# One table load for both blocks' norms, and Newton steps one slot later, in a decoder block on one NeuronCore

## The chip, the cores and the metric

The kernel runs on one core of one Trainium2 chip. The metric is the device time of one execution in microseconds, the lower the better. TensorE multiplies, ScalarE applies activation functions (each function needs its table in the engine, and a table is brought in by an ACT_TABLE_LOAD in ScalarE's own queue), VectorE and GpSimd do elementwise work, and SyncE issues every DMA of this kernel.

## The reference, cut to what matters

One layer over 2048 positions of 1024 features: a norm and an input projection into two token mixers (gated linear attention and a short convolution), an output projection with residual, and then the part that this change touches:

```
def rmsnorm(x, g):
    y = xf * lax.rsqrt(jnp.mean(xf * xf, axis=-1, keepdims=True) + NORM_EPS)
    return (y * g).astype(x.dtype)
...
        x = x + mixed
        h2 = rmsnorm(x, norm2_g[l])
        ffn = (jax.nn.silu(h2 @ w_ffn_gate[l]) * (h2 @ w_ffn_up[l])) @ w_ffn_down[l]
        x = x + ffn
    return rmsnorm(x, norm_f_g)
```

All of it is float32; D_FF is 2816.

## The kernel before, in words

**Tiling.** Features lie on partitions (128 of them, 8 tiles), positions on the free axis in four blocks of 512. The FFN goes over two halves of two blocks each: `ffn_up(0)`, `ffn_down(0)`, `ffn_up(1)`, `ffn_down(1)`. In `ffn_up` a step m (11 of them) makes two units, one for the gate weights and one for the up weights.

**A unit** (L370) multiplies a 2 by 2 matrix of weight tiles with a 2 by 2 matrix of operand tiles with seven products instead of eight (Strassen and Winograd). Every float32 value is split into a high and a low part (`split`, L152: ScalarE copies the high part, L153, VectorE subtracts to get the low one, L154), and each product takes 12 matmuls in `ffn_up`: four feature tiles times high·high, high·low and low·high (L366 to L368). The third matmul of a product is the first that needs the low half of its weights. The seven weight combinations are named A11, S1, S2, A12, S3, S4 and A22, in the order in which their splits are written (L343); GpSimd makes the sums (L349 to L356). Results stay in PSUM and ScalarE (L386) and VectorE (L390) take them out. The last product, with A22, adds onto the bank of the product with S3, so that it can start only when VectorE has read that bank into the tile called c22. Four buffers hold split weights, eight PSUM banks are shared by everything.

**Order of the work.** Each engine runs its queue strictly in the order in which the program's scheduler put it. `tick` (L201) is called after every product: every second tick gives one step to the background list (in `ffn_up` the splits and stores of the activations, `split_later`), and of the ticks between, every second one gives a step to the list `ahead`. One such step is called a slot here; it comes every four products.

**The norms made beside the projections** are steps of `ahead`:

- `h2_ahead` (L864), beside `ffn_up(0)`: the second norm of the two blocks of half 1. For block j after two slots each, `psum_rstd` (L175) multiplies the squares' sums with a matrix of ones on TensorE (`tot`), and `finish_rstd` (L182) takes Ln (L184) and Exp (L185) on ScalarE for a first guess y0 of the inverse root, scales `tot` on VectorE (L186), and improves the guess with a Newton step, three VectorE instructions (`newton`, L162: L163 to L165). The result lies in PSUM as `rb_ps`. Then `combine` makes the operands of half 1.
- `finish_later` (L976), beside `ffn_up(1)`: the final norm of the two blocks of half 0. For each block: eight slots that load a tile and add its square (`sum_squares`, L770), one `psum_rstd`, eight slots that load, scale (L992) and store a tile.

The Silu of the gate units (`silu`, L420, instruction L422) needs another table than Ln and Exp.

Of the kernel before, what the change touches and what calls it, by code (L numbers as in the profile page):

```python
# [10 lines left out]
F32 = mybir.dt.float32  # L11
F32R = mybir.dt.float32r
U32 = mybir.dt.uint32
AF = mybir.ActivationFunctionType
ALU = mybir.AluOpType
# [3 lines left out]
P = 128  # L19
D = 1024  # L20
SEQ = 2048
PB = 512
# [9 lines left out]
EPS = 1e-6  # L32
# [14 lines left out]
C_G1, C_G2, C_GF, C_BG, C_GN, C_CW = 0, 8, 16, 24, 26, 27  # L47
# [4 lines left out]
def tile_hymba_block(ctx, tc, x, xt, win, wa, wgu, wout, wffn, wdown, wdown_first, small, out):  # L52
    nc = tc.nc
    act, dve, pool, pe = nc.scalar, nc.vector, nc.gpsimd, nc.tensor

    def pool_of(name, bufs, **kw):
        return ctx.enter_context(tc.tile_pool(name=name, bufs=bufs, **kw))
# [6 lines left out]
    tiny = pool_of("tiny", 2)  # L64
# [11 lines left out]
    ones = const.tile([P, P], F32, name="ones")  # L76
# [8 lines left out]
    eps = const.tile([P, 1], F32, name="eps")  # L85
# [46 lines left out]
    def col(c):  # L132
        return sml[:, c : c + 1]

    def bank(name="mm"):
        return ps.tile([P, PB], F32, name=name, tag="mm")

    def tt(name):
        return tp.tile([P, PB], F32, name=name, tag="t")

    def bt(name, shape=(P, PB)):
        return bx[0].tile(list(shape), F32, name=name, tag="b")

    def load(dst, src):
        return nc.sync.dma_start(dst, src)

    def store(dst, src):
        return nc.sync.dma_start(dst, src)
# [13 lines left out]
    def newton(y, v, l, y0):  # L162
        dve.tensor_tensor(l, y0, y0, ALU.mult)  # L163
        dve.scalar_tensor_tensor(l, l, -0.5, v, ALU.mult, ALU.mult)
        dve.scalar_tensor_tensor(y, l, 1.5, y0, ALU.add, ALU.mult)  # L165
# [6 lines left out]
        finish_rstd(rb, tot, n)  # L172
        return rb

    def psum_rstd(ssq, n):  # L175

        tot, rb = bank("tot"), bank("rb_ps")
        pe.matmul(tot[:], ones[:], ssq[:], start=True, stop=True)
        finish_rstd(ssq, tot, n, rb)
        return rb  # L180

    def finish_rstd(v, tot, n, rb=None):  # L182
        l, y0 = bt("l"), bt("y0")
        act.activation(l[:], tot[:], AF.Ln, bias=eps[:], scale=1.0 / n)  # L184
        act.activation(y0[:], l[:], AF.Exp, scale=-0.5)  # L185
        dve.tensor_scalar(v[:], tot[:], 1.0 / n, EPS, ALU.mult, ALU.add)  # L186
        newton((v if rb is None else rb)[:], v[:], l[:], y0[:])
# [227 lines left out]
        act.activation(s[:], c[:], AF.Copy)  # L415
        return s

    last_silu = []

    def silu(c, in_psum):  # L420
        s = tt("sg") if in_psum else c
        last_silu[:] = [act.activation(s[:], c[:], AF.Silu)]  # L422
        return s


# [170 lines left out]
    def in_proj(half, ops, first=None, differences=None):  # L596
# [20 lines left out]
        for i0 in (0, 2):  # L617
            for r, j, c, p in next(units):
                store(s_g[2 * half + j][i0 + r][:], silu(c, p)[:])
# [150 lines left out]
    def sum_squares(ssq, y, first):  # L770
        if first:
            act.activation(ssq[:], y, AF.Square)
        else:
            q = tt("q")
            act.activation(q[:], y, AF.Square)  # L775
            pool.tensor_tensor(ssq[:], ssq[:], q[:], ALU.add)  # L776

    def build_mix(half):
        def pair(b, k):
            return load_pair(s_gla[b][:, k] if k < HEADS else s_mix[b][k - HEADS])  # L780

        return [[pair(2 * half + j, k) for j in range(2)] for k in range(KD)]
# [81 lines left out]
    def h2_ahead(ssq):  # L864


        rb = []
        for j in range(2):
            for _ in range(2):
                yield  # L870
            rb.append(psum_rstd(ssq[j], D))

        def put(n, k, h):
            store_split(s_h2p[n][k], h)

        yield from combine(lambda k, j: s_x1[2 + j][k][:], C_G2, rb, put)
# [34 lines left out]
    def store_split(dst, y):  # L911
        o = bx[1].tile([P, 2, PB], F32R, name="so", tag="so")
        split(y[:], o[:, 0, :], o[:, 1, :])
        store(dst[:], o[:].bitcast(F32))
# [6 lines left out]
    def ffn_down(half):  # L921
# [51 lines left out]
        if half == 0:  # L973
            ahead[:] = [finish_later(half)]

    def finish_later(half):  # L976

        for j in range(2):
            ssq = tiny.tile([P, PB], F32, name="ssx0", tag="ssx0", bufs=1)
            for d in range(KD):  # L980
                y = bt("y")
                load(y[:], s_x1[2 * half + j][d][:])
                yield
                sum_squares(ssq, y[:], d == 0)
            yield
            act.preload_act_table_set("natural_log_exp_and_others")
            rb = psum_rstd(ssq, D)
            for d in range(KD):
                y = bt("y")
                load(y[:], s_x1[2 * half + j][d][:])  # L990
                yield
                dve.scalar_tensor_tensor(y[:], y[:], col(C_GF + d), rb[:], ALU.mult, ALU.mult)  # L992
                store(out[2 * half + j, :, d, :], y[:])

    def last_unit(src, ops, b12, y, ssq):
# [71 lines left out]
    ssq = out_proj(0, build_mix(0))  # L1067
    drain_background(lambda: (3, PT - 1) in done)
    h2 = no_operands()
    ssq = out_proj(1, build_mix(1), h2_first(ssq, h2), h2_rest(h2))  # L1070
    ahead.append(h2_ahead(ssq))
    mixing.close()
    bx[:] = [
# [112 lines left out]
```

## Time and profile before

| | |
|---|---|
| runs of the kernel | 2110.91 us median of 3 (2108.93 to 2113.38) |
| profiled execution | span 2109.1 us from its first to its last instruction; no other time is recorded of it |
| TensorE busy | 2033.1 us, 96% |
| VectorE busy | 1418.4 us, 67% |
| ScalarE busy | 1014.1 us, 48% |
| GpSimd busy | 972.4 us, 46% |
| mean granted TensorE clock | 0.992 of full |

A row of the waits names the engine and line that stood still, the engine and line that ended it, and then the total in us, the number of times and the longest one. A row of the timeline gives start, duration, engine, line, operation and tiles, and in brackets the idle time before it and who ended it. A row of the windows gives, after the stretch, the busy us of TensorE, of its weight loads, of VectorE, ScalarE and GpSimd, each with the number of instructions, then the granted clock, the DMA share and GB/s. In the profile TensorE is PE, VectorE DVE, ScalarE ACT, GpSimd POOL.

### The profile page before, as it was taken

To read this page: it belongs to the slowest core of one execution; us is meant where nothing else is said; L and a number is where in the kernel's file an instruction comes from. 1 tells how busy PE (TensorE), PEld (TensorE's weight loads), DVE (VectorE), ACT (ScalarE), POOL (GpSimd) and SP (SyncE) were. 2 spreads that over 40 slices of the span, in tenths; PEclk is the share of its full clock that TensorE was granted. 3 is DMA by queue.
4 is the path that set the end of the run, shared out by engine and by line. 5 is a ranking of instruction groups with operands and counts; after the bars stand their busy time and mean duration, and the time that the engine had idled before them with its cause. 6 is when DMAs were issued, how large, how long until landed. Compare 5 with 4: busy or idle time off the path is not lost.

```text
span 2109.1 us, 26874 instructions
## 1 busy us (share of the span) xinstructions
PE 2033.1 (96%) x9133; PEld 1648.9 (78%) x9133; DVE 1418.4 (67%) x1983; ACT 1014.1 (48%) x1997; POOL 972.4 (46%) x703
## 2 busy tenths in 40 slices
PE   5999999999999999999999999999999989999996
PEld 4778888877888878788888878787888868877775
DVE  7669786549753786788786665554766666665564
ACT  5555455656542356445545443333554554543344
POOL 3436322222102464564464348764645544436774
PEclk9999999999999999999999999999999999999998
DMA  7349485425586872656545687697454535587763
GB/s 277 126 158 318 139 329 164 148 83 164 201 284 235 325 249 100 241 198 221 217 172 220 243 327 272 235 338 296 158 207 179 206 134 190 183 344 281 269 269 110
DMA packets 189241, 464.43 MB, mean 220 GB/s; under 512 B 19824, under 2 KB 65072, under 8 KB 179504
## 3 DMA queue, kind: packets, MB, share of 16 engines
q1 hardware_dynamic: 189104, 462.72, 60.4%
q8 instruction: 72, 1.18, 0.2%
q14 instruction: 65, 0.53, 0.1%
HBM read 297.49 MB, written 165.15 MB: 219 GB/s over the span
## 4 chain that ended last, share of the span: by engine, by line
PE 70%; DVE 8%; DMA 7%; ACT 3%; issue 3%; POOL 2%; SPq 0%; DVEq 0%; ACTq 0%; POOLq 0%
PE mm L366 21%; PE mm L368 21%; PE mm L367 21%; DVE wq L154 2%; DMA op<-shT 1%; DVE so L154 1%; PE mm L794 1%; DVE h L490 1%; PE mm L795 1%; PE mm L797 1%; DVE op L154 1%; DMA sx<-y 1%; ACT wq L153 1%; PE o_ps L718 1%; DMA shT<-so 1%
## 5 line engine op out<-in xcount | busy, mean ns | idle before, releaser
L366 PE MATMUL mm<-op,wq 128*128 128x512 f32 x2499 | 981.3, 395 | 23.8 <-DVE c L390 7.8
L368 PE MATMUL mm<-op,wq 128*128 128x512 f32 x2499 | 966.1, 392 | 12.6 <-DVE wq L154 11.9
L367 PE MATMUL mm<-op,wq 128*128 128x512 f32 x2499 | 976.0, 391 | 0.0
L154 DVE TENSOR_TENSOR wq<-raw,wq 128x512 fp32r<-128x512 f32 (+2 forms) x626 | 527.3, 849 | 329.9 <-ACT wq L153 324.3
L153 ACT ACTIVATE wq<-raw 128x512 fp32r<-128x512 f32 (+2 forms) x626 | 363.6, 587 | 555.8 <-PE mm L368 402.4
L366 PEld LDWEIGHTS mm<-op,wq 128*128 128x128 f32 x2499 | 470.8, 188 | 137.6 <-ACT wq L153 12.3
L368 PEld LDWEIGHTS mm<-op,wq 128*128 128x128 f32 x2499 | 470.5, 188 | 123.5 <-DVE wq L154 24.8
L367 PEld LDWEIGHTS mm<-op,wq 128*128 128x128 f32 x2499 | 471.2, 189 | 96.7 <-issue 1.0
L351 POOL TENSOR_TENSOR raw<-s,raw 128x512 f32<-128x512 f32 (+2 forms) x97 | 127.5, 1314 | 422.2 <-DVE wq L154 402.0
L390 DVE TENSOR_TENSOR c<-mm,c 128x512 f32<-128x512 f32 x267 | 183.0, 686 | 95.7 <-PE mm L368 93.0
L349 POOL TENSOR_TENSOR s<-raw 128x512 f32<-128x512 f32 (+2 forms) x97 | 130.2, 1343 | 216.2 <-DMA raw<-in_wffn_dram 88.8
L356 POOL TENSOR_TENSOR raw<-raw 128x512 f32<-128x512 f32 (+2 forms) x97 | 126.7, 1306 | 135.3 <-DVE wq L154 128.1
L386 ACT ACTIVATE c<-mm 128x512 f32<-128x512 f32 x267 | 154.7, 585 | 38.0 <-PE mm L368 36.8
L776 POOL TENSOR_TENSOR ssx<-ssx,q 128x512 f32<-128x512 f32 x52 | 76.5, 1483 | 156.0 <-ACT q L775 155.8
L350 POOL TENSOR_TENSOR raw<-raw 128x512 f32<-128x512 f32 (+2 forms) x97 | 135.1, 1393 | 4.1
L965 POOL TENSOR_TENSOR y<-c,y 128x512 f32<-128x512 f32 x66 | 98.7, 1499 | 49.0 <-DVE c L390 46.6
L154 DVE TENSOR_TENSOR so<-t,so 128x512 fp32r<-128x512 f32 x100 | 91.2, 918 | 25.9 <-ACT so L153 25.4
L153 ACT ACTIVATE wq<-s 128x512 fp32r<-128x512 f32 (+2 forms) x97 | 56.9, 586 | 93.5 <-PE mm L368 83.3
L794 PE MATMUL mm<-op,wq 128*128 128x512 f32 x256 | 100.9, 395 | 0.0
L795 PE MATMUL mm<-op,wq 128*128 128x512 f32 x256 | 99.8, 390 | 0.0
L154 DVE TENSOR_TENSOR wq<-s,wq 128x512 fp32r<-128x512 f32 (+2 forms) x97 | 84.1, 867 | 15.6 <-ACT wq L153 15.0
L153 ACT ACTIVATE so<-t 128x512 fp32r<-128x512 f32 x100 | 62.5, 627 | 41.8 <-DMA sa_T<-so 16.1
(177 smaller groups left out, 1885.0 us busy)
## 6 DMA issues: line engine op xcount, KB each, us to landing
raw<-in_wffn_dram SPq DMA_DIRECT2D x44, 1024.0 KB, 5.7
sa_T<-so SPq DMA_DIRECT2D x88, 512.0 KB, 5.3
op<-sa_T SPq DMA_DIRECT2D x88, 512.0 KB, 9.2
sa_B<-so SPq DMA_DIRECT2D x69, 512.0 KB, 3.4
op<-sa_B SPq DMA_DIRECT2D x69, 512.0 KB, 9.0
raw<-in_win_dram SPq DMA_DIRECT2D x23, 1024.0 KB, 5.5
raw<-in_wdown_dram SPq DMA_DIRECT2D x24, 768.0 KB, 6.2
sx<-y SPq DMA_DIRECT2D x48, 256.0 KB, 3.2
```

Of the source, the lines that this page charges most:

```text
L153: last_hi[:] = [act.activation(hi, src, AF.Copy)]
L154: return dve.tensor_tensor(lo, src, hi.bitcast(F32), ALU.subtract)
L349: pool.tensor_tensor(s1, a21, a22, ALU.add)
L350: pool.tensor_tensor(a21, a11, a21, ALU.subtract)
L351: pool.tensor_tensor(a11, s1, a11, ALU.subtract)
L356: pool.tensor_tensor(a12, a12, a11, ALU.subtract)
L366: pe.matmul(o[:], wh, xh, start=first and k == 0, stop=False, skip_group_check=True)
L367: pe.matmul(o[:], wh, xl, start=False, stop=False, skip_group_check=True)
L368: return pe.matmul(o[:], wl, xh, start=False, stop=k == n - 1, skip_group_check=True)
L386: act.activation(t[:], o[:], AF.Copy)
L390: dve.tensor_tensor(t[:], o[:], t[:], ALU.add)
L794: pe.matmul(o[e, j][:], wh, m[:, 0, :], start=k == 0, stop=False)
```

## The change

`psum_rstd` goes, and `both_rstd` treats the two blocks together: two `tot` products, one load of the table that holds Ln and Exp (asked for behind the last Silu issued), two Ln, two Exp and two scalings; then one slot of `ahead` passes, and then come both Newton steps. Every Ln, Exp and later Silu is tied behind the one before it, so that the scheduler can't mix them. `h2_ahead` waits three slots and does both blocks in the fourth and fifth, where the old one did them in the third and fifth. `finish_later` sums the squares of both blocks first (16 slots), makes both norms, and then scales both blocks; the second block's factor waits in SBUF and is copied by ScalarE into a PSUM bank when its turn comes.

```
-    def psum_rstd(ssq, n):
-        tot, rb = bank("tot"), bank("rb_ps")
-        pe.matmul(tot[:], ones[:], ssq[:], start=True, stop=True)
-        finish_rstd(ssq, tot, n, rb)
-        return rb
+    def both_rstd(ssq, rb):
+        tot = [bank("tot") for _ in range(2)]
+        for j in range(2):
+            pe.matmul(tot[j][:], ones[:], ssq[j][:], start=True, stop=True)
+        l, y0 = [[bt(n) for _ in range(2)] for n in ("l", "y0")]
+        with tc.issue_after(last_silu[0].ins):
+            last_exp[:] = [act.preload_act_table_set("natural_log_exp_and_others")]
+        for j in range(2):
+            with tc.issue_after(last_exp[0].ins):
+                last_exp[:] = [
+                    act.activation(l[j][:], tot[j][:], AF.Ln, bias=eps[:], scale=1.0 / D)
+                ]
+        for j in range(2):
+            with tc.issue_after(last_exp[0].ins):
+                last_exp[:] = [act.activation(y0[j][:], l[j][:], AF.Exp, scale=-0.5)]
+        for j in range(2):
+            dve.tensor_scalar(ssq[j][:], tot[j][:], 1.0 / D, EPS, ALU.mult, ALU.add)
+        yield
+        for j in range(2):
+            newton((rb[j] or ssq[j])[:], ssq[j][:], l[j][:], y0[j][:])
...
     def silu(c, in_psum):
         s = tt("sg") if in_psum else c
-        last_silu[:] = [act.activation(s[:], c[:], AF.Silu)]
+        with ExitStack() as stack:
+            if last_exp:
+                stack.enter_context(tc.issue_after(last_exp[0].ins))
+            last_silu[:] = [act.activation(s[:], c[:], AF.Silu)]
...
     def h2_ahead(ssq):
-        rb = []
-        for j in range(2):
-            for _ in range(2):
-                yield
-            rb.append(psum_rstd(ssq[j], D))
+        for _ in range(3):
+            yield
+        rb = [bank("rb_ps") for _ in range(2)]
+        yield from both_rstd(ssq, rb)
...
     def finish_later(half):
+        ssq = [
+            tiny.tile([P, PB], F32, name=f"ssx{j}", tag=f"ssx{j}", bufs=1) for j in range(2)
+        ]
         for j in range(2):
-            ssq = tiny.tile([P, PB], F32, name="ssx0", tag="ssx0", bufs=1)
             for d in range(KD):
                 y = bt("y")
                 load(y[:], s_x1[2 * half + j][d][:])
                 yield
-                sum_squares(ssq, y[:], d == 0)
-            yield
-            act.preload_act_table_set("natural_log_exp_and_others")
-            rb = psum_rstd(ssq, D)
+                sum_squares(ssq[j], y[:], d == 0)
+        yield
+        rb = [bank("rb_ps"), None]
+        yield from both_rstd(ssq, rb)
+        for j in range(2):
+            if j:
+                rb[1] = bank("rb_ps")
+                act.activation(rb[1][:], ssq[1][:], AF.Copy)
             for d in range(KD):
                 y = bt("y")
                 load(y[:], s_x1[2 * half + j][d][:])
                 yield
-                dve.scalar_tensor_tensor(y[:], y[:], col(C_GF + d), rb[:], ALU.mult, ALU.mult)
+                dve.scalar_tensor_tensor(y[:], y[:], col(C_GF + d), rb[j][:], ALU.mult, ALU.mult)
                 store(out[2 * half + j, :, d, :], y[:])
```

In the built programs TensorE has 8869 matmuls and transposes and SyncE 1233 DMAs, before and after; ScalarE has 1911 instructions before and 1904 after: eight table loads fewer and one copy more. The order moves at three places.

**First place, ScalarE beside `ffn_up(0)`,** where the second of the two h2 norms was. In the rows, c11 and c12 are results of a gate unit that Silu works on, `wq` a split weight quarter (7836 is A11 and 7842 S1 of the next unit), l and y0 the norm's tiles. Before:

```order
L386 ACTIVATE c12_7744<-mm_7698 128x512
L153 ACTIVATE wq_7836<-raw_7833 128x512
L422 ACT_TABLE_LOAD
L422 ACTIVATE c11_7711<-c11_7711 128x512
L184 ACT_TABLE_LOAD
L184 ACTIVATE l_7779<-tot_7776,eps_97 128x512
L185 ACT_TABLE_LOAD
L185 ACTIVATE y0_7780<-l_7779 128x512
L153 ACTIVATE wq_7842<-s1_7835 128x512
L422 ACT_TABLE_LOAD
L422 ACTIVATE c12_7744<-c12_7744 128x512
```

The same stretch of ScalarE after (7837 is the A11 that was 7836; the load for Ln and Exp stands 13 instructions earlier, behind the last Silu of the unit before):

```order
L153 ACTIVATE so_7765<-sg_7521 128x512
L186 ACTIVATE l_7706<-tot_7702,eps_97 128x512
L186 ACTIVATE l_7707<-tot_7703,eps_97 128x512
L153 ACTIVATE wq_7681<-raw_7659 128x512
L401 ACTIVATE c22_7736<-mm_7719 128x512
L190 ACTIVATE y0_7708<-l_7706 128x512
L190 ACTIVATE y0_7709<-l_7707 128x512
L153 ACTIVATE wq_7684<-raw_7659 128x512
L401 ACTIVATE c12_7750<-mm_7687 128x512
L153 ACTIVATE wq_7837<-raw_7834 128x512
L440 ACT_TABLE_LOAD
L440 ACTIVATE c11_7717<-c11_7717 128x512
```

The first block's norm, which stood some 20 instructions ahead with two loads of its own, has moved down to the second one, and both stand ahead of the unit's end with no load among them.

**Second place, VectorE beside `ffn_up(1)`,** at the final norm of the second block (c22 is read from the bank that the product with A22 adds onto). Before:

```order
L154 TENSOR_TENSOR wq_15015<-s1_15008,wq_15015 128x512
L186 TENSOR_SCALAR ssx0_14197<-tot_14988 128x512
L154 TENSOR_TENSOR so_15146<-t4_14843,so_15146 128x512
L163 TENSOR_TENSOR l_14991<-y0_14992 128x512
L390 TENSOR_TENSOR c22_14908<-mm_14876,c22_14908 128x512
L164 SCALAR_TENSOR_TENSOR l_14991<-l_14991,ssx0_14197 128x512
```

After, both blocks' final norms stand in an up unit some 420 matmuls ahead of that place:

```order
L192 TENSOR_SCALAR ssx1_12749<-tot_14195 128x512
L163 TENSOR_TENSOR l_14198<-y0_14200 128x512
L163 TENSOR_TENSOR l_14199<-y0_14201 128x512
L164 SCALAR_TENSOR_TENSOR l_14198<-l_14198,ssx0_12748 128x512
L405 TENSOR_TENSOR c22_14130<-mm_14095,c22_14130 128x512
L164 SCALAR_TENSOR_TENSOR l_14199<-l_14199,ssx1_12749 128x512
L154 TENSOR_TENSOR wq_14250<-raw_14238,wq_14250 128x512
L165 SCALAR_TENSOR_TENSOR rb_ps_14193<-l_14198,y0_14200 128x512
```

At the old place nothing of a norm is left, and at the new one c22 has four instructions of the two norms right ahead of it, where it had two, with one of other work between them.

**Third place, TensorE at the old place of that norm.** Rows are matmuls; 14866 is S3, 14873 A22, both of one gate unit. Before:

```order
L367 MATMUL mm_14876<-op_12688,wq_14866 128x512
L368 MATMUL mm_14876<-op_12688,wq_14866 128x512
L366 MATMUL mm_14876<-op_12698,wq_14873 128x512
L367 MATMUL mm_14876<-op_12698,wq_14873 128x512
```

After (14874 is S3 of the same unit, 15010 is A11 of the next):

```order
L382 MATMUL mm_14884<-op_12689,wq_14874 128x512
L383 MATMUL mm_14884<-op_12689,wq_14874 128x512
L381 MATMUL mm_15035<-op_12651,wq_15010 128x512
L382 MATMUL mm_15035<-op_12651,wq_15010 128x512
```

Before, the product with A22 followed the one with S3 directly; after, two products (24 matmuls) of the next unit stand between them, as they do in the other units of `ffn_up`. At the new place of the final norms the two products stand there as well. Elsewhere the order moves a little: three loads of `combine` go ahead of one load of weights on SyncE, the loads of the second block's tiles go ahead of the first block's stores, GpSimd's sums of squares follow them, and in the first two groups of `ffn_down(1)` some products change places.

More of the change, by code (lines that the diff above doesn't have):

```diff
@@ L416, in settled @@
         return s
-    last_silu = []
+    last_silu, last_exp = [], []
     def silu(c, in_psum):
         s = tt("sg") if in_psum else c
-        last_silu[:] = [act.activation(s[:], c[:], AF.Silu)]
+        with ExitStack() as stack:
+            if last_exp:
+                stack.enter_context(tc.issue_after(last_exp[0].ins))
+            last_silu[:] = [act.activation(s[:], c[:], AF.Silu)]
         return s
```

## Prediction

> **What bounds the kernel now.** I read the page first: which engine fills the span, and which one the chain of work that ended last runs through.
>
> ```profile
> span 2109.1 us, 26874 instructions
> ...
> PE 2033.1 (96%) x9133; PEld 1648.9 (78%) x9133; DVE 1418.4 (67%) x1983; ACT 1014.1 (48%) x1997; POOL 972.4 (46%) x703
> ...
> PE 70%; DVE 8%; DMA 7%; ACT 3%; issue 3%; POOL 2%; SPq 0%; DVEq 0%; ACTq 0%; POOLq 0%
> ```
>
> TensorE is busy 96% of the span, and ScalarE, whose work the change cuts, 48%. Shorter ScalarE work is therefore worth nothing by itself; it is worth time only where TensorE stands still for it. So the second view is TensorE's waits over the whole span, the third the `tot` products of the norms (first and last start), and the fourth the windows at and behind them.
>
> ```profile
> PE mm L368 <- DVE wq L154: 11.9, 11, 2.5
> PE mm L366 <- DVE c L390: 7.8, 2, 7.2
> ```
>
> ```profile
> L178 PE MATMUL tot<-ssx,ones x8: 591/592/592, 808.3 to 1716.6; 128*128 128x512 f32 x8
> ```
>
> ```profile
> 800.00:820.00 20.00, 20.00 (x88) 16.20 (x87) 11.56 (x17) 10.55 (x16) 4.10 (x3) 1.00 0.21 79
> 840.00:860.00 20.00, 17.15 (x67) 13.31 (x67) 20.00 (x25) 11.71 (x22) 12.01 (x8) 0.91 0.53 200
> 1520.00:1540.00 20.00, 20.00 (x88) 16.20 (x87) 16.37 (x23) 17.47 (x28) 7.49 (x6) 1.00 0.68 245
> 1720.00:1740.00 20.00, 12.80 (x51) 10.47 (x52) 9.98 (x15) 11.73 (x18) 4.15 (x3) 0.83 0.44 163
> ```
>
> Four norms are made beside the projections, the h2 pair from 808.3 us on and the final pair up to 1716.6. At the first of each pair TensorE never stops: 800 to 820 and 1520 to 1540 hold 88 matmuls each, the full number. Behind the second of each it loses: 67 matmuls from 840 to 860 and 51 from 1720 to 1740, with a lower granted clock in both. The longest single wait of each of the two quoted kinds, 2.5 and 7.2 us, falls there. These two holes are all that the change can fill.
>
> **How large the holes are.** The timeline of TensorE at both:
>
> ```profile
> 846.39 0.39 PE L367 MATMUL mm<-op,wq 128*128 128x512 f32 x1
> 849.28 0.72 PE L368 MATMUL mm<-op,wq 128*128 128x512 f32 x1 [2.51 <-DVE wq L154]
> ...
> 852.79 0.41 PE L367 MATMUL mm<-op,wq 128*128 128x512 f32 x1
> ```
>
> ```profile
> 1719.37 0.39 PE L367 MATMUL mm<-op,wq 128*128 128x512 f32 x1
> 1719.60 0.39 PE L368 MATMUL mm<-op,wq 128*128 128x512 f32 x1
> 1727.19 0.79 PE L366 MATMUL mm<-op,wq 128*128 128x512 f32 x1 [7.21 <-DVE c L390]
> ...
> 1730.21 0.40 PE L367 MATMUL mm<-op,wq 128*128 128x512 f32 x1
> ```
>
> One matmul starts 0.23 us after the one before (1719.37 to 1719.60; 20.00 us over 88 gives 0.227). At the first place the start at 849.28 comes 2.89 us after 846.39, which loses 2.89 − 0.23 = 2.66. The next eight starts, up to 852.79, take 3.51 us where 8 × 0.227 = 1.82 would do: 1.69 lost to the lower clock. Together 4.35; the window has it a little larger, 88 − 67 = 21 matmuls of 0.227 us, **4.8 us**, and I take that. At the second place 1719.60 to 1727.19 loses 7.59 − 0.23 = 7.36, and the seven starts up to 1730.21 take 3.02 instead of 1.59, which loses 1.43: **8.8 us** (the window: 37 × 0.227 = 8.4). Both together, 13.6 us, are the most that the change can give.
>
> [...]
>
> **Why the holes are there.** ScalarE and VectorE at the first place, then ScalarE and VectorE at the second:
>
> ```profile
> 833.83 1.28 ACT L184 ACT_TABLE_LOAD   x1
> 835.12 0.69 ACT L184 ACTIVATE l<-tot,eps 128x512 f32<-128x512 f32 x1
> 835.84 1.28 ACT L185 ACT_TABLE_LOAD   x1
> 837.13 0.63 ACT L185 ACTIVATE y<-l 128x512 f32<-128x512 f32 x1
> ```
>
> ```profile
> 835.85 0.69 DVE L186 TENSOR_SCALAR ssx<-tot 128x512 f32<-128x512 f32 x1 [3.26 <-ACT l L184]
> 837.79 0.69 DVE L163 TENSOR_TENSOR l<-y 128x512 f32<-128x512 f32 x1 [1.25 <-ACT y L185]
> ...
> 846.88 2.35 DVE L154 TENSOR_TENSOR wq<-raw,wq 128x512 fp32r<-128x512 f32 x2
> ```
>
> ```profile
> 1721.30 1.28 ACT L184 ACT_TABLE_LOAD   x1
> ...
> 1723.82 1.28 ACT L185 ACT_TABLE_LOAD   x1
> 1725.12 0.63 ACT L185 ACTIVATE y<-l 128x512 f32<-128x512 f32 x1
> ```
>
> ```profile
> 1725.78 0.76 DVE L163 TENSOR_TENSOR l<-y 128x512 f32<-128x512 f32 x1 [1.17 <-ACT y L185]
> 1726.46 0.68 DVE L390 TENSOR_TENSOR c<-mm,c 128x512 f32<-128x512 f32 x1
> ```
>
> VectorE's queue is in order. At the first place its scaling L186 waits 3.26 us for Ln and its first Newton instruction 1.25 us for Exp, because a load of 1.28 us stands ahead of either in ScalarE's queue. That makes VectorE 4.5 us late, and in the next 20 us it is busy all the time (20.00 in the window); the low half of A12 ends at 849.23 (846.88 + 2.35), where TensorE, at its full pace, wanted it at 846.39 + 0.23 = 846.62: 2.6 us late. At the second place c22 stands behind the first Newton instruction, which waits for Exp behind two loads. The matmul with A22 needs c22 read, and in this unit it follows the product with S3 directly, so TensorE has nothing else to do from 1720.0 until c22 ends at 1727.14.
>
> **The change, part by part.**
>
> *Second place.* Nothing of a norm is left there, and the order of TensorE puts two products, 24 × 0.227 = 5.4 us of work, between S3 and A22. c22 then needs 0.68 us plus what little stands ahead of it, so the wait goes, and with it the slow starts: **−8.8 us**. The next thing in line is the Silu's bank of the same unit, which is the ordinary course of the other units, where TensorE is full.
>
> *The new place of the final pair.* Here a new wait could arise. The same unit before:
>
> ```profile
> 1623.93 0.69 DVE L390 TENSOR_TENSOR c<-mm,c 128x512 f32<-128x512 f32 x1 [0.70 <-PE mm L368]
> ...
> 1631.86 0.69 DVE L894 TENSOR_TENSOR sg<-mm,sg 128x512 f32<-128x512 f32 x1 [3.38 <-PE mm L368]
> ```
>
> The row at 1623.93 is c22, and the product with A22 that needs it ends at 1631.86; 12 matmuls of 0.227 earlier it began, at about 1629.1. In the new order the second `tot` comes right ahead of the product with S3, and VectorE does one scaling, two squares and one more Newton instruction ahead of c22: four times about 0.6 us (the rows at 1725.78 and 1726.46 start 0.68 apart), 2.7 us, after ScalarE's Ln (0.69) and two Exp (0.63 each, as in the rows above) have run behind `tot`, without a load. These 2.0 us of ScalarE run while TensorE does the product with S3, 12 × 0.227 = 2.7 us, which c22 has to await anyway. So c22 moves back by at most 2.7 us of the 1629.1 − 1623.93 − 0.69 = 4.5 us that it has. I take **0**; the bounds are 0 and, if c22 came as late as at the old place (7.4 us behind the product with S3, against the 5.4 that two products give), 2.0.
>
> *First place.* ScalarE has the load 13 instructions ahead of the first Ln, so Ln, Ln, Exp, Exp take 2 × 0.69 + 2 × 0.63 = 2.6 us for both norms, where one took from 833.83 to 837.76, 3.9 us. VectorE's waits of 3.26 and 1.25 us shrink to those for single activations, under 0.7 each. VectorE then comes to A12 up to 4.5 us sooner, against 2.6 needed. Against that stand one first-block norm more in this stretch (its four VectorE instructions, 4 × 0.6 = 2.4 us, stood before in the window from 800 to 820, where TensorE did not wait) and the single waits, about 1 us; it also has the idle time before the pair. The margin is 4.5 − 2.6 − 1 = 0.9 us, less whatever of the 2.4 us doesn't fit ahead of the busy stretch. I take off 0.8 us as a remainder: **−4.0 us**, with bounds of 0 (VectorE as late as now) and −4.8.
>
> *Table loads.* Eight loads of 1.28 us go, 10.3 us of ScalarE, and a copy of one tile comes, about as long as an Exp, 0.6 us. All of it lies beside TensorE, which has 88 of 88 matmuls wherever ScalarE is not late: **0**, but for what the places above already count. Without that cover the copy would cost its 0.6.
>
> *Totals, DMAs, GpSimd.* Four `tot` products stay four. The three loads that pass a weight load on SyncE, and the sums of squares that move on GpSimd, carry the same work in the same number of slots, and neither queue ends a wait of TensorE in these windows: **0**. A weight load held up behind them would show as a wait of ScalarE's copies; I put its bound into the 2.3 us below.
>
> *The changed order in `ffn_down(1)`.* From 1740 to 2060 TensorE waits in the old order:
>
> ```profile
> PE mm L366 <- ACT wq L153: 2.5, 2, 1.5
> PE mm L366 <- DVE y L390: 0.8, 1, 0.8
> ```
>
> The longest of the first kind and the one of the second, 1.5 + 0.8 = 2.3 us, stand where products change places. They may go or come a second time: 0, between −2.3 and +2.3.
>
> **The sum.** −8.8 − 4.0 = −12.8 us: the span falls from 2109.1 to 2096.3. The median of the runs, 2110.91, lies 1.8 us above the span, so I expect a median of **2098.1 us**, 0.6% less.
>
> **The rivals.**
>
> *A: only the second place pays.* VectorE's load in the busy stretch stays and the first-block norm joins it, so that A12 is as late as now. For it: 20.00 us busy of 20 from 840 to 860. Against it: the 4.5 us of idle waits in front go for certain. Time: 2110.9 − 8.8 = 2102.1.
>
> *B: a new hole at the new place of the final pair, or in `h2`'s.* VectorE's queue gets eight norm instructions in a row; if c22 or a low half is late by a wait with the slow clock behind it, such as the 2.66 + 1.69 of the first place, at one place, and the first place keeps its 4.8 us, the gain is 8.8 − 4.4 = 4.4: 2106.5, and 2108.8 with 2.3 us lost in `ffn_down(1)`. For it: L186 waits for Ln (3.26 us above), and so the two scalings hold VectorE twice. Against: the two products between, 5.4 us.
>
> *C: slower.* The pair stalls as one lump. At the dear place one norm held TensorE for 7.4 us; if two norms hold it twice as long at the new place, 14.7 us and 1.4 for the clock, and the first place keeps its 4.8, the sum is 16.1 − 8.8 = +7.3: 2118.2. It decides from the point where c22 comes more than 5.4 us behind the product with S3, and turns the sign from 8.8 us beyond that. Against it: the old 7.4 us were two loads and an A22 without products ahead of it, and both are gone in the new order.
>
> [...]
>
> **How the numbers follow.** The forecast (both places paid, within 3 us of 2098.1) gets 0.65; it needs no new wait, and all three orders point the same way. A gets 0.15, B 0.13, C 0.07. The range goes from 2093.5 (all 13.6 and the 2.3 of `ffn_down(1)` off 2110.9 would give 2095.0, less half the 3 us or so by which single runs differ from the median) to 2106, which takes in A and leaves out C and most of B, under 0.2. What a measurement of this kernel tells from no change is about 0.2%, 4.2 us. Faster by more: the forecast, A and a little of B, 0.83. Within: most of B, 0.10. Slower: C, 0.07.
>
> **What would show it.** In the profile after, TensorE's wait for L390 of 7.2 us should be gone, and 0.6 us at most of that kind remain; the windows at the old second place should hold 88 matmuls in 20 us with the clock at 1.00. At the first place the wait for `wq` of 2.5 us should be under 1. ScalarE should show eight loads fewer, and VectorE's waits for Ln L186 should be 1 us or less. The forecast is wrong if TensorE stands over 2 us in the unit where the final pair is now made, if the wait for A12's low half stays near 2.5 us, or if the order in `ffn_down(1)` costs more than 2.3 us.

## The result and the profile after

The changed kernel takes 2102.39 us (median of 5 runs, 2099.06 to 2105.63) against 2110.80 (5 runs, 2108.88 to 2113.38): a ratio of 0.9961, with a 95% interval of 0.9949 to 0.9973. It was timed twice more beside the kernel before, with ratios of 0.9960 (0.9947 to 0.9974) and 0.9951 (0.9939 to 0.9963). The gain is thus some 8 to 10 us where 12.8 were forecast. The profiled execution has a span of 2100.5 us. One run of the kernel with all loads kept, below, took 5991.5 us and is left out of its median.

The page of the changed kernel, and TensorE's waits over its whole span (engine and line that stood still, who ended it: total us, times, longest):

```profile
span 2100.5 us, 26873 instructions
...
PE 2034.6 (97%) x9133; PEld 1649.8 (79%) x9133; DVE 1420.2 (68%) x1983; ACT 1003.2 (48%) x1990; POOL 971.9 (46%) x703
```

```profile
PE mm L383 <- DVE wq L154: 9.6, 7, 2.7
PE mm L381 <- ACT wq L153: 7.4, 7, 1.8
...
PE mm L381 <- ACT c L401: 6.6, 7, 2.6
...
PE mm L381 <- DVE c L405: 0.6, 1, 0.6
```

ScalarE has 7 instructions and 10.9 us less: eight loads gone, one copy come. The wait of 7.2 us for c22 is gone (L405 is the old L390). What came in its stead is in the second row: the longest wait for ScalarE's weight copies was 1.5 us and is 1.8.

The windows of the changed kernel at the old place of the second h2 norm, at the new place of the final pair (two rows), at the old place of the second final norm (work lies some 2 us earlier ahead of it and 11 us behind it), and in `ffn_down(1)`:

```profile
840.00:860.00 20.00, 19.00 (x81) 14.73 (x80) 20.00 (x25) 10.74 (x19) 10.74 (x7) 1.00 0.67 237
1600.00:1620.00 20.00, 20.00 (x86) 15.86 (x85) 12.45 (x20) 12.71 (x23) 6.76 (x5) 1.00 0.55 191
1620.00:1640.00 20.00, 20.00 (x90) 16.56 (x89) 18.75 (x23) 8.75 (x15) 11.19 (x7) 1.00 0.32 128
1710.00:1730.00 20.00, 20.00 (x89) 16.38 (x89) 13.03 (x21) 9.39 (x18) 5.82 (x4) 1.00 0.72 250
1920.00:1940.00 20.00, 18.24 (x79) 14.22 (x78) 11.46 (x16) 5.97 (x12) 17.05 (x14) 1.00 0.35 114
```

TensorE is full at the old second place (89 matmuls where 51 stood) and at the pair's new place. From 840 to 860 it has 81 instead of 67, with the clock at 1.00, but not the full 88. From 1920 to 1940 it stands for 1.76 us, and there GpSimd is the busy engine (17.05 of 20 us).

**Where the time went, place by place.** All these kernels have 9133 rows of TensorE matmuls in the profile, so the time between the nth and the mth can be set against the same two of the kernel before, which takes out of the comparison whatever differs ahead of the place. The table is worked out so, in us against the profiled execution of the kernel before; the stretches are named by its own times. The changed kernel was profiled three times (C1 the result's, C2 and C3 the experiments'), the kernel before a second time (B2).

```
stretch               B2     C1    C2    C3    what lies there
 800 to  870         0.0   -3.2  -3.2  -3.2   first place (h2 norms)
1500 to 1700         0.0   +0.7  +0.6  +0.7   new place of the final pair
1700 to 1740        +0.3   -9.2  -9.3  -8.7   second place
1910 to 1960         0.0   +1.9  +1.9  +1.5   ffn_down(1), changed order
2030 to 2060        +1.6   +1.6  +1.6  +1.6   a wait of 2.6 in all; half clock behind it
```

Stretches that the change does not touch differ too, by up to 2.7 us between executions of the same kernel (B2 from 0 to 800). A total (a `tot` product) is two rows and costs TensorE 0.4 us more than two other matmuls (in C1 the third start behind the one at 1611.28 is at 1612.37, 1.09 us later, where three matmuls take 0.68). One total left the second place and two stand in the stretch from 1500 to 1700, which had one, so the second place itself gives −8.7, and the new place costs 0.3. The four places that the change touches sum to −3.2 + 0.7 − 9.1 + 1.8 = **−9.8 us**, which all three intervals hold.

The last row is not the change's: the unaltered kernel has it too when it is profiled again. It comes back under the hardware.

### The profile page after: what moved, and what is told of

Same layout as the page of the kernel before. It is cut to its first block, busy times and chain, and to the rows that moved or that the text cites. A ratio compares the mean times of both kernels' runs of the same rounds, so it can differ in the third digit from the quotient of the medians.

```text
span 2100.5 us, 26873 instructions
## 1 busy us (share of the span) xinstructions
PE 2034.6 (97%) x9133; PEld 1649.8 (79%) x9133; DVE 1420.2 (68%) x1983; ACT 1003.2 (48%) x1990; POOL 971.9 (46%) x703
## 4 chain that ended last, share of the span: by engine, by line
PE 74%; DVE 10%; DMA 8%; issue 3%; POOL 3%; ACT 3%; SPq 0%; DVEq 0%; POOLq 0%; ACTq 0%
PE mm L381 22%; PE mm L383 22%; PE mm L382 22%; DVE wq L154 2%; DVE h L508 2%; PE mm L812 1%; DVE op L154 1%; PE mm L813 1%; PE mm L815 1%; DVE so L154 1%; DMA raw<-in_wffn_dram 1%; DMA raw<-in_wdown_dram 1%; DMA op<-shT 1%; PE a_ps L576 1%; DVE c L405 1%
## 5 line engine op out<-in xcount | busy, mean ns | idle before, releaser
L366 POOL TENSOR_TENSOR raw<-s,raw 128x512 f32<-128x512 f32 (+2 forms) x97 | 127.6, 1316 | 422.6 <-DVE wq L154 402.5
L405 DVE TENSOR_TENSOR c<-mm,c 128x512 f32<-128x512 f32 x267 | 183.0, 685 | 94.4 <-PE mm L383 92.1
```

Source lines behind the costliest of these rows:

```text
L366: pool.tensor_tensor(a11, s1, a11, ALU.subtract)
L405: dve.tensor_tensor(t[:], o[:], t[:], ALU.add)
```

## The experiments

Each was timed beside the kernel before in five rounds, whose median was 2112.6, 2113.1 and 2112.3 us in the three sets. The line numbers shift by a few from kernel to kernel; each row is named by what it does.

**The changed kernel again, and the kernel before again** (no edit):

> The changed kernel unaltered, profiled a second time. Theory (two holes paid, the rest is a clock that drops at other short waits): 2102.4 again within 3 us; the holes at both old places stay away, the new wait of about 1.8 us for ScalarE's weight copies in ffn_down(1) is there again, since the order is the same, while some of the half-clock stretches behind waits of 1.5 to 2.7 us (785, 1232 and 2037 us in the first profile) stand elsewhere or are missing. Rival (the change itself makes the three new half-clock stretches): all three are at the same places again, and no other appears.

> The kernel before unaltered, profiled a second time. Theory (half-clock stretches land by chance on waits of 1.5 to 2.7 us): the waits at about 786, 847, 1235, 1720 and 2048 us are the same as in the first profile within 0.3 us, but at least one of 786, 1235 and 2048 us, which ran at full clock there, shows a half-clock stretch of 3.4 us, or the one at 849 us is missing. Rival (the stretches belong to the program): 849 and 1723 us have them and 786, 1235 and 2048 have none. The time is 2110.8 by both, and its median against the first one shows what this measurement can tell apart.

2103.33 us and a ratio of 0.9960 for the one, 2112.72 and 1.0003 (0.9991 to 1.0014) for the other: an unaltered kernel is told from itself to within some 0.1%. The three places of the change and the wait in `ffn_down(1)` repeat within 0.6 us. The half-clock stretches do not: of C1's at 785, 1232 and 2037 us, C2 has only the last, C3 the first and the last and one more at 1875, and the unaltered kernel now has one at 2046 where it had none. As the theory had it, the half-clock stretches away from the two old holes come and go between executions, so a single profile can't put them down to the change.

**Half of the change each.** Only the h2 pair (the final norms as in the kernel before), and only the final pair (h2 as before):

```
     def finish_later(half):
...
-        rb = [bank("rb_ps"), None]
-        yield from both_rstd(ssq, rb)
...
+            rb = psum_rstd(ssq, D)
```

```
     def h2_ahead(ssq):
...
-        yield from both_rstd(ssq, rb)
...
+            rb.append(psum_rstd(ssq[j], D))
```

> Only the h2 pair is made at once, the final norms as before. Theory: the first place pays alone, -3.2 to -4.0 us, the hole of 7.4 us behind the second final norm stays, and the order in ffn_down(1) is the old one, so no new wait there: 2107 to 2108. Rival (the gain is ScalarE's shorter work, and half of the eight loads go here): half of the 8.4 us, 2106.6; told from the theory by TensorE's wait for L390 of 7 us alone. Rival (only the second place pays, the first place's change is chance): 2110.8.

> Only the final pair is made at once, the h2 norms as before. Theory: -8.7 us at the second place, the first place keeps its wait of 2.5 us for the low half of A12, and ffn_down(1), whose products stand in the changed kernel's order here, has the new wait of about 2 us: 2110.8 - 8.7 + 2 = 2104.1. Rival (the gain goes by the loads removed, half of them here): 2106.6. Rival (the order in ffn_down(1) costs nothing): 2102.

2108.43 us, 0.9979 (0.9968 to 0.9989), and 2105.03 us, 0.9962 (0.9948 to 0.9976). TensorE's waits of the h2 kernel from 1700 to 1740, then those of the final kernel from 800 to 870 and from 1900 to 1960:

```profile
PE mm L388 <- DVE c L412: 7.2, 1, 7.2
```

```profile
PE mm L390 <- DVE wq L154: 2.9, 2, 2.5
```

```profile
PE mm L388 <- ACT wq L153: 1.7, 1, 1.7
```

Each half keeps the hole of the other. By places the h2 kernel has −3.2 from 800 to 870 and nothing in `ffn_down(1)`; the final one has −8.3 at the second place, +0.6 at the new one and +1.9 in `ffn_down(1)`, −5.8 by sum (its first place is 1.0 shorter as well, because no half clock follows the wait there; see the hardware). Both sums lie in the intervals (−6.8 to −2.3 and −11.0 to −5.1). The h2 half's 4.2 us would be the share of half the loads as well, but the final half's 7.6 is not, and each hole goes with its own place: the rival of ScalarE's shorter work as such falls. The new wait in `ffn_down(1)` comes with the order of products: it is there (1.7 or 1.8 us) in every kernel of this study that has the changed order, and in none with the old one, whatever else was edited.

**The changed kernel with all loads kept.** Ln, Exp, Ln, Exp, each behind a load, in the changed places and with TensorE's order unaltered:

```
-        with tc.issue_after(last_silu[0].ins):
-            last_exp[:] = [act.preload_act_table_set("natural_log_exp_and_others")]
+        last_exp[:] = last_silu
         for j in range(2):
...
-        for j in range(2):
             with tc.issue_after(last_exp[0].ins):
                 last_exp[:] = [act.activation(y0[j][:], l[j][:], AF.Exp, scale=-0.5)]
```

> The changed kernel with its pairs and its slot, but each Ln and each Exp loads its table as in the kernel before: Ln, Exp, Ln, Exp with a load of 1.28 us ahead of each, in place of one load for the four. TensorE's order of products is exactly that of the changed kernel. Theory (the place pays at the final pair, the loads pay at h2): the old second place stays free, the wait of 2.5 us for A12's low half and its half clock come back at h2 (+4), and at the final pair's new place the four loads (5.1 us) against the two products' 5.4 us cost 0 to 2.4: 2106 to 2109. Rival (only place and order count, the loads lie beside TensorE everywhere): 2102.4. Rival (the loads are the whole gain): 2110.8.

2106.35 us (median of the ten other runs), 0.9974 (0.9964 to 0.9984): 3.0 us above the changed kernel in the same set, as the theory had it. ScalarE at h2 with the loads kept, and TensorE there:

```profile
826.58 1.28 ACT L188 ACT_TABLE_LOAD   x1
827.88 0.63 ACT L188 ACTIVATE y<-l 128x512 f32<-128x512 f32 x1
828.52 1.28 ACT L185 ACT_TABLE_LOAD   x1
829.82 0.69 ACT L185 ACTIVATE l<-tot,eps 128x512 f32<-128x512 f32 x1
```

```profile
836.10 0.50 PE L381 MATMUL mm<-op,wq 128*128 128x512 f32 x1 [1.04 <-DVE wq L154]
840.83 0.50 PE L381 MATMUL mm<-op,wq 128*128 128x512 f32 x1 [1.67 <-DVE wq L154]
849.78 0.50 PE L379 MATMUL mm<-op,wq 128*128 128x512 f32 x1 [0.94 <-ACT c L399]
873.50 0.50 PE L379 MATMUL mm<-op,wq 128*128 128x512 f32 x1 [1.64 <-ACT c L399]
```

In place of the single hole of 2.51 us there are smaller ones: two waits for low halves and one for ScalarE's copy in the stretch, of whose −3.2 only −0.3 us is left, and a fourth just behind it (it belongs to the next stretch). At the final pair the same loads cost nothing: +0.5 at the new place, −9.3 at the old one. So at h2 there is no gain while the loads stay, and at the final norms the place pays whether they stay or not.

**The kernel before with its second final norm one slot later**, loads and all:

```
     def finish_later(half):
         for j in range(2):
...
             yield
+            if j:
+                yield
```

> The kernel before with one thing altered: the second final norm comes one slot of the background work later, and with all its loads. Its tot product then stands ahead of the product with S3 of the next unit's second block, where two products lie between S3 and A22 as everywhere else. Theory (the dear place was dear by the products that follow, not by the loads alone): the wait of 7.2 us falls under 1.5, -6 to -8.8 us, and ffn_down(1), whose order becomes that of the changed kernel, gives 2 back: 2104 to 2107. Rival (two loads ahead of Exp stall VectorE wherever they stand): 2110.8.

2105.03 us, 0.9962 (0.9948 to 0.9975). VectorE there, with the scaling L186 and the first Newton instruction L163 waiting for Ln and Exp as before, and TensorE's waits for c22 over the whole span:

```profile
1732.08 0.69 DVE L186 TENSOR_SCALAR ssx<-tot 128x512 f32<-128x512 f32 x1 [0.71 <-ACT l L184]
1734.02 0.69 DVE L163 TENSOR_TENSOR l<-y 128x512 f32<-128x512 f32 x1 [1.25 <-ACT y L185]
...
1737.16 0.68 DVE L390 TENSOR_TENSOR c<-mm,c 128x512 f32<-128x512 f32 x1
```

```profile
PE mm L366 <- DVE c L390: 0.6, 1, 0.6
```

The norm itself is as slow as ever: the first Newton instruction waits the same 1.25 us behind a load. But two products lie between S3 and A22 in this unit, and TensorE has no wait at all from 1700 to 1790. The cover is close: c22 ends at 1737.84, and by the starts of the matmuls the product with S3 ends at about 1732.6, so c22 comes 5.2 us behind it, where the two products give 5.4. One `yield` gives −8.9 us at the second place, as much as the whole rebuilding of the final pair. Its total is that of the final pair alone, too.

**The kernel before with one load for each norm**, neither pair nor slot:

```
-    def finish_rstd(v, tot, n, rb=None):
+    def finish_rstd(v, tot, n, rb=None, tied=False):
...
+            if tied:
+                with tc.issue_after(last_silu[0].ins):
+                    last_exp[:] = [act.preload_act_table_set("natural_log_exp_and_others")]
...
```

> The kernel before with separate norms at (nearly) their old slots, but each with one load of the common table, put behind the last Silu, and no pair and no slot between. Theory: at h2 the single norm's 3.9 us on ScalarE becomes about 1.3 behind the load, VectorE is under 2 us late, the wait of 2.5 us goes: -3 to -4; at the second final norm the 7.4 us of hole held two loads of 1.28 ahead of Exp, one of which goes and the other runs ahead of tot: 7.4 - 2.6 = 4.8 us of hole stay; ffn_down(1) has the changed kernel's order, +2: 2110.8 - 3.5 - 2.6 + 2 = 2106.7. Rival (loads are the whole gain, the pair is only its form): 2102.4. Rival (place alone counts): 2110.8 or more.

2111.21 us, 0.9996 (0.9985 to 1.0007): no gain that can be told from none, where the theory had 4. Its waits from 1700 to 1740 and from 800 to 870:

```profile
PE mm L378 <- DVE c L402: 4.3, 1, 4.3
```

```profile
PE mm L380 <- DVE wq L154: 2.1, 1, 2.1
```

The second place is as expected, 4.3 us of hole (4.8 forecast). The first is not: the low half of A12 is still 2.1 us late instead of on time, and of what the stretch gains (−2.7) 1.6 us is half clock that does not follow here. That is not because VectorE still waits for loads. Its scaling and the first instruction behind the Newton steps:

```profile
829.87 0.69 DVE L198 TENSOR_SCALAR ssx<-tot 128x512 f32<-128x512 f32 x1 [0.17 <-ACT l L189]
...
835.40 0.75 DVE L505 SCALAR_TENSOR_TENSOR h<-h,sml,rb_ps 128x512 f32<-128x512 f32 x1 [1.84 <-DMA h<-sx]
```

The waits of 3.26 us for Ln and 1.25 for Exp have shrunk to 0.17 and nothing, and Newton ends some 5 us sooner against TensorE's work. But VectorE then stands 1.84 us for a DMA that brings h, and A12's low half comes only 1.1 us sooner. So the loads alone do not explain the first hole; which part of the changed order spares the rest, the pair or its later place, is not separated here. Elsewhere a new wait of 1.0 us for ScalarE's copy arises at the first final norm (+2.1 from 1500 to 1700), and `ffn_down(1)` costs 1.5. In sum, fewer loads at the old places are worth nothing that can be measured: most of what they gain at the two places is lost at the two others.

**The slot.** Without it at both pairs; with it behind the Newton steps instead of ahead; without it at the final pair only:

```
-        yield
         for j in range(2):
             newton((rb[j] or ssq[j])[:], ssq[j][:], l[j][:], y0[j][:])
+        yield
```

(This is the second of them. In the first and the third the `yield` stays in its place, but behind a condition that does not hold: `if False`, and a parameter that is false for the final pair.)

> The changed kernel without the slot between the exponentials and the Newton steps, which then follow the scalings directly. ffn_down(1) has the old kernel's order of products here. Theory: VectorE waits for Ln and Exp in a row, 2.6 us, with c22 behind it; the two products after S3 (5.4 us) hide that: 0 at the final pair, and at h2 up to +2; the wait of 1.8 us in ffn_down(1) goes, -2: 2100 to 2103. Rival (the slot is what saves the first place): the wait for A12's low half comes back with 2 us or more and the time is 2104 to 2107.

> The changed kernel with the slot put behind the Newton steps instead of ahead of them, at both pairs: as many slots as the changed kernel has from there on. Theory, formed on the kernel without the slots (which lost 2.4 us each at 831, 932, 1010 and 1087 us to waits for ScalarE's copies that stood behind the copies of h2): the number of slots decides what of h2 stands ahead of those copies, so the waits are gone and at most 2 us for VectorE's wait on Ln and Exp come: 2102 to 2105. Rival (the Newton steps must come a slot later, whatever follows): the waits of 2 us stay, 2109 to 2112.

> The changed kernel with its slot at h2, but without the slot at the final pair, where the Newton steps follow the scalings directly. ffn_down(1) then has the order of products of the kernel before. Theory (the new order in ffn_down(1) costs 2 us; the loss without any slot was h2's): the wait of 1.7 us for ScalarE's weight copies at about 1930 us is gone, -2; a wait of 1.1 us for ScalarE's copy of a block at about 1650 us, which the kernel without both slots shows, may come, +1: 0.1% to 0.5% and more under the kernel before, 2099 to 2102 where the changed kernel gave 2102.4 to 2103.3. Rival (the slot at the final pair is needed): 2106 or more.

Without the slots 2111.26 us, 0.9999 (0.9988 to 1.0009): the whole gain is gone, and my expectation of 2100 to 2103 was wrong. ScalarE and TensorE at h2 without the slot:

```profile
824.65 1.15 ACT L190 ACTIVATE y<-l 128x512 f32<-128x512 f32 x2
825.75 0.63 ACT L153 ACTIVATE wq<-raw 128x512 fp32r<-128x512 f32 x1
830.89 0.63 ACT L153 ACTIVATE so<-h 128x512 fp32r<-128x512 f32 x1 [4.50 <-DVE h L509]
...
832.98 1.06 ACT L402 ACTIVATE c<-mm 128x512 f32<-128x512 f32 x2
```

```profile
833.61 0.50 PE L382 MATMUL mm<-op,wq 128*128 128x512 f32 x1 [2.52 <-ACT c L402]
```

I had looked at VectorE's queue, and the damage is in ScalarE's. Newton steps that come at once bring the copies of h2 (`so<-h`) into ScalarE's queue a slot sooner. The first of them stands there for 4.50 us, until VectorE has done Newton and scaled h, and the copy of a product's bank that TensorE needs is behind it. Three more waits for such copies, of 1.6 to 1.9 us, come up at 932, 1011 and 1090 us, since all that follows is a slot early as well.

The slot behind the Newton steps tells these apart: 2107.38 us, 0.9974 (0.9963 to 0.9985). The three later waits are gone (870 to 1200: −2.1 against +2.6), and the one at the pair is not:

```profile
833.16 0.63 ACT L153 ACTIVATE so<-h 128x512 fp32r<-128x512 f32 x1 [4.55 <-DVE h L508]
```

```profile
835.88 0.66 PE L381 MATMUL mm<-op,wq 128*128 128x512 f32 x1 [3.22 <-ACT c L401]
```

I had expected at most 2 us there; it is 3.22, and with the half clock behind it the first place loses 2.3 where the change gains 3.2. So both readings were half right: the number of slots decides the later waits, the slot ahead of Newton the one at h2.

Without the slot at the final pair alone: 2103.60 us, 0.9959 (0.9945 to 0.9972). `ffn_down(1)` is back in its old order and free of its wait, but from 1500 to 1700 it loses 2.8 instead of 0.7, 1.4 of it this wait:

```profile
PE mm L382 <- ACT c L402: 1.4, 1, 1.4
```

I had expected 2099 to 2102. Instead it is level with the changed kernel, as what the one place gains the other loses.

**The final pair one slot earlier**, and the changed kernel beside it:

```
             sum_squares(ssq[j], y[:], d == 0)
-        yield
         rb = [bank("rb_ps"), None]
```

> The changed kernel with the final pair and all behind it one slot of the background earlier (the slot ahead of its totals is left out, the one between exponentials and Newton steps kept). The two totals then stand inside products of the unit, and ffn_down(1) has the order of the kernel before. Theory: the wait at about 1930 us is gone, -2, and no hole arises at the totals: 2099 to 2102. Rival (the place of the totals in the unit is what pays): a wait of 1 to 3 us for c22 at about 1620 us, 2102 to 2106.

> The changed kernel unaltered, timed beside the three others of this set: 2102 to 2104 by both theories. It is there for the difference of the kernel without the slot at the final pair, which by the theory lies 1 to 3 us under it and by the rival 3 us or more above.

2106.14 us, 0.9966 (0.9952 to 0.9979), and 2102.05, 0.9951 (0.9939 to 0.9963). The old order in `ffn_down(1)` saves its 1.8, and the stretch from 1500 to 1700 loses 6.0 us. The rival was right on the size and wrong on the cause: no wait for c22, but a low half late behind VectorE's splits, with half clock behind it:

```profile
1636.11 0.50 PE L383 MATMUL mm<-op,wq 128*128 128x512 f32 x1 [2.35 <-DVE wq L154]
```

No version beats the changed kernel; whatever freed `ffn_down(1)` at the final pair paid for it between 1600 and 1700.

## Why the prediction was right, and where it was too large

The measured 2102.39 us lies inside the stated range, but 4.3 us above the 2098.1 and so outside the 3 us around it that the forecast gave itself. By time alone the run would speak for the rival A; the places speak against it.

*Second place, −8.8 us:* right in size and in mechanism. The stretch shows −9.1, of which 0.4 is the total that left. The single slot shows that the place does it, with the two products between S3 and A22 as cover; the loads alone were worth 2.9 of the 7.2 us of wait (7.2 against 4.3 with one load, which also runs ahead).

*First place, −4.0 us:* −3.2 in three executions out of three. The hole itself is filled, as forecast: −4.6 us by the matmul that started at 853 in the kernel before. The mechanism is half shown. With the loads kept the gain is gone, but without them at the old place the low half was still 2.1 us late, so the step "VectorE then comes to A12 up to 4.5 us sooner" did not follow from the shorter waits for Ln and Exp alone. The remainder of 0.8 was put in the wrong place: no wait for A12's low half remained at all; instead two for ScalarE's copies, of 0.33 and 0.54 us, came to the front and take 1.4 us by the starts of the matmuls. In the changed kernel:

```profile
847.62 0.63 ACT L153 ACTIVATE wq<-raw 128x512 fp32r<-128x512 f32 x1 [0.92 <-POOL raw L371]
848.16 1.07 ACT L401 ACTIVATE c<-mm 128x512 f32<-128x512 f32 x2
```

A weight copy waits there for a sum of GpSimd, with the bank's copy behind it. The hole of 2.51 us had covered that.

*New place of the final pair, 0:* +0.3, inside its bounds, and TensorE does not wait there. VectorE's waits for Ln are gone at h2 as forecast: its two scalings and its first two Newton instructions start without one.

```profile
827.94 1.27 DVE L192 TENSOR_SCALAR ssx<-tot 128x512 f32<-128x512 f32 x2
829.14 0.68 DVE L154 TENSOR_TENSOR wq<-raw,wq 128x512 fp32r<-128x512 f32 x1
829.74 1.28 DVE L163 TENSOR_TENSOR l<-y 128x512 f32<-128x512 f32 x2
```

That the slot is a condition for it (without it +2.4 to +2.8 in all from 1500 to 1700, and h2 lost) the prediction did not say.

*Table loads, 0:* right beyond the places. *Totals, DMAs and GpSimd, 0:* right for the totals (0.4 each, only moved). For GpSimd it was wrong in one stretch that it had not looked at, the next.

*The changed order in `ffn_down(1)`, 0 ± 2.3:* +1.8, inside its bounds but **the term that was furthest off**. GpSimd, ScalarE and TensorE there in the changed kernel:

```profile
1926.05 1.33 POOL L365 TENSOR_TENSOR raw<-raw 128x384 f32<-128x384 f32 x1
1927.35 1.28 POOL L989 TENSOR_TENSOR y<-x,y 128x512 f32<-128x512 f32 x1
1928.59 0.99 POOL L366 TENSOR_TENSOR raw<-s,raw 128x384 f32<-128x384 f32 x1
```

```profile
1929.61 1.35 ACT L153 ACTIVATE wq<-raw 128x384 fp32r<-128x384 f32 x3 [0.55 <-POOL raw L366]
```

```profile
1930.18 0.50 PE L381 MATMUL mm<-op,wq 128*128 128x512 f32 x1 [1.76 <-ACT wq L153]
```

The same two sums of GpSimd in the kernel before (L351 is the old L366, L972 the old L989):

```profile
1938.46 1.01 POOL L351 TENSOR_TENSOR raw<-s,raw 128x384 f32<-128x384 f32 x1
1939.43 1.29 POOL L972 TENSOR_TENSOR y<-x,y 128x512 f32<-128x512 f32 x1
```

The sum of the weights (L366) stands in GpSimd's queue behind a sum of the residual (L989) that stood behind it before. Against TensorE's work it starts 1.84 us later, while TensorE's own matmuls up to there are in step to 0.01 us. All 14 profiled executions agree: where the residual's sum stands ahead the matmul waits, and where it stands behind it does not. The bound was right and the middle was not: I took it as equally likely to gain or to lose.

Together: 0.8 + 1.8 + 0.3 = 2.9 of the 3.0 us between −12.8 and −9.8.

**Rivals.** A (only the second place pays) came nearer in time, 2102.1, but not by its mechanism: both places paid. B and C needed the pair to stall VectorE with c22 or a low half behind it. The changed kernel shows neither. Low halves that are late by over 1 us come in two of its variants, with the loads kept at h2 and with the final pair a slot earlier; without the slot it was ScalarE's copies that stalled.

## What to carry to other kernels

A hole in front of the busiest engine is priced by what its queue holds next: where two products more stood ahead of the one that waits, a norm with all its loads cost nothing (TensorE has no wait from 1700 to 1790 with the second final norm one slot later), so look first for an order with more work between before making the slow thing faster. When a step is moved, follow its outputs into every queue that takes them up, not only the one that was late; here the copies behind the Newton steps undid the whole gain when they came a slot early (2111.26 us without the slots). And a new order further on has a price of its own, which is looked for in the queue of the engine that feeds the weights there.

## What the runs showed of the hardware

In these traces a wait of 2 to 3 us had half clock behind it in some executions and not in others. The same wait of 2.51 us at the first place, in the kernel before and in the one with the final pair only, each in two windows of 3.4 us (TensorE's busy time is the second number, the clock the one after the five busy times):

```profile
846.00:849.40 3.40, 0.89 (x5) 0.43 (x4) 3.40 (x4) 2.27 (x4) 2.09 (x3) 1.00 0.94 329
849.40:852.80 3.40, 3.40 (x9) 2.63 (x10) 3.40 (x3) 1.80 (x4) 3.26 (x2) 0.50 0.38 155
```

```profile
846.10:849.50 3.40, 2.01 (x9) 1.31 (x7) 3.40 (x3) 1.47 (x3) 3.27 (x3) 1.00 0.96 340
849.50:852.90 3.40, 2.25 (x10) 1.80 (x10) 3.40 (x5) 1.31 (x3) 2.22 (x2) 1.00 0.61 247
```

In the kernel before the granted clock is 0.50 in the second window, and 1.7 us are lost there by the starts of the matmuls; with the final pair only, where the wait lies in both windows (1.4 and 1.2 us idle), it is 1.00 in both. Not all of the 1.7 us is gained then: the first place of the two kernels that have the wait without the half clock (the final pair only, and the single slot) is 1.0 us shorter than in the kernel before, and a wait of 0.3 us for ScalarE's copy shows there. The wait of 2.6 us near 2045, in the two executions of the unaltered kernel:

```profile
2044.10:2047.50 3.40, 1.43 (x7) 0.85 (x5) 1.75 (x3) 2.54 (x6) 2.55 (x2) 1.00 0.00 0
2047.50:2050.90 3.40, 2.77 (x12) 2.31 (x13) 0.79 (x2) 2.07 (x5) 3.23 (x3) 1.00 0.63 226
```

```profile
2042.90:2046.30 3.40, 0.81 (x4) 0.35 (x2) 1.85 (x4) 2.57 (x6) 2.91 (x3) 1.00 0.00 0
2046.30:2049.70 3.40, 3.39 (x8) 2.72 (x9) 0.68 (x1) 1.05 (x2) 3.02 (x3) 0.50 0.68 231
```

In the first execution the clock is 1.00 in both windows; in the second it is 0.50 behind the wait, and by the table the stretch from 2030 to 2060 takes 1.6 us more. Why the same wait has half clock behind it in one execution and not in the other is not settled here.

So a wait of 2 to 3 us cost some 1.7 us of slow clock on top in some executions and nothing in others. In the prediction 1.69 of the first place's 4.35 us were of this kind. The second place's 7.2 us had half clock behind them in the kernel before (1.43 us lost), and its second execution took 0.3 us more from 1700 to 1740; whether half clock always follows there is not shown. The profiled half-clock stretches elsewhere differ from execution to execution (from 200 to 2060 us, away from the two old holes, the kernel before had one and three, the changed one four, two and four), and whether the changed kernel pays part of its gain back there by more than chance these counts cannot settle.
